# A two-layer attention and convolution encoder on one Trainium2 core: separate buffers for the convolution's first two accumulators

## The chip, the core and the metric

The kernel runs on one core of a Trainium2 chip. The core has a matrix engine (TensorE, in the profile PE, its weight loads PEld), a vector engine (VectorE, DVE), an activation engine (ScalarE, ACT), GpSimd (POOL), which here only issues transfers, and SyncE (SP), which issues the weight loads. Each engine works through its own queue in the order in which the program was written out for it. The metric is the device time of one execution, in microseconds; less is better.

## What is computed

Two layers over 512 tokens of width 1024, all in float32. Each layer is

```
x += 0.5 * SwiGLU(RMSNorm(x))
h  = RMSNorm(x); z = h @ W_in + b_in
     z = [q | k | v (3 head groups) | GLU input | 2 gates]
     A: dilated sliding-window attention of 3 groups, combined, projected
     B: u = a * sigmoid(g) -> depthwise convolution over 31 tokens -> LayerNorm -> Silu -> projected
x += (sigmoid(gate_A) * A + sigmoid(gate_B) * B) @ W_out
x += 0.5 * SwiGLU(RMSNorm(x))
x  = RMSNorm(x)
```

The change lies in branch B. The reference's convolution is, for each of the 1024 channels, a sum of 31 shifted and scaled copies of `u`, plus a bias.

## The kernel before, in words

Activations lie transposed, channels on the 128 partitions and the 512 tokens along the row, so that 1024 channels are eight tiles of 128x512. Every matrix product is made of three matmuls: both factors are split into a high and a low part (`hi`, `lo`; `xgh`, `xgl`; `zh`, `zl`), and `mm3` (lines 156 to 159) adds high x high, high x low and low x high in PSUM. Weights come in through `stage` (lines 140 to 154): SyncE loads 512 KB into `raw` (two buffers), ScalarE writes `hi` (line 152), VectorE writes `lo` (line 153; four buffers each).

`mixer` (from line 264) runs once a layer and does, in program order:

1. The GLU (lines 277 to 292): four chunks of two channel tiles. `ps_gg` and `ps_ga` are projected, scaled on VectorE (lines 287, 290), the gate goes through Sigmoid (line 288), and line 292 writes `u[k]`.
2. Three head groups: `tables` (lines 326 to 328), `qk_chunk` (lines 331 to 372), `v_chunk` and `attend` (lines 403 to 471). A unit of `attend` is scores on TensorE (424), a masked minimum on VectorE (437), Exp on ScalarE (443), transposes (446), a copy (448) and the product with V (454).
3. The two gates (lines 482 to 504), projected from the same `xgh`, `xgl` as the GLU and put through Sigmoid.
4. The convolution (lines 507 to 517), on VectorE alone: for each `k`, line 510 begins an accumulator `cv[k]` from `u[k]`, and line 516 adds the other 30 taps, one instruction each.
5. The LayerNorm over channels (lines 518 to 536): sum of the `cv` (520, 522), mean by a matmul with ones (524), subtraction (529), squares (184, 188), their sum (193), square root and reciprocal (198, 200), broadcast (207, 209), scaling (534), Silu (535), and the split of the result into `zh` and `zl` (166, 167). These two are written into the tags `xgh{k}` and `xgl{k}`, of which there is one buffer each.
6. The combination of the head groups (lines 539 to 578), whose results `y` are split into tiles of the tag `big`.
7. The projections of both branches (`ps_cp`, `ps_ap`), the merge, and the output projection.

The order on each engine is not the program's. A scheduler writes it out at compile time by a model of its own: an instruction with a smaller priority number (earlier in the program) goes first among those that are ready in the model, and later ones fill the holes. Two calls shift it: `stage` moves its three steps ahead by 150, and the LayerNorm (line 518) gets the priority of the point before the attention units, so that it goes ahead of units that are still waiting. A tile is taken from a ring of as many buffers as its tag has, and tiles of one tag take their buffers in program order; a tile whose buffer still has a reader waits for it. In the mixer the tag `big` serves `u[0]` to `u[7]`, then `cv[0]` to `cv[7]`, then the eight tiles of `y`, in this order, from `NB` = 10 buffers:

```
u[k] = slot("big", NB, name="u")                 # line 291
a = slot("big", NB, name="cv")                   # line 509
y.append(split(mp, acc, "big", NB))              # line 578
```

Of the kernel before, what the change touches and what calls it, by code (L numbers as in the profile page):

```python
# [44 lines left out]
def trunk(ctx: ExitStack, tc: tile.TileContext, A: dict, out: bass.AP):  # L45
# [79 lines left out]
    def pc(nm, l, k):  # L125
        i = VECS.index(nm) * 16 + l * 8 + k
        return pcol[:, i:i + 1]

    def cw(l, j, k):
        i = (l * CW + j) * 8 + k  # L130
        return cwc[:, i:i + 1]
# [4 lines left out]
    def uniq(s):  # L136
        cnt[0] += 1
        return f"{s}_{cnt[0]}"
# [22 lines left out]
    def split(pool, src, tag, bufs):  # L161

        return split_to(pool.tile([P, S], F32R, tag=tag, name=uniq("sh"), bufs=bufs), pool.tile([P, S], F32R, tag=tag, name=uniq("sl"), bufs=bufs), src)
# [100 lines left out]
    def mixer(l, xg, R, rr, after):  # L264
# [5 lines left out]
        with ExitStack() as mx:  # L270
            mp = mx.enter_context(tc.tile_pool(name=uniq("mix"), bufs=2))

            def slot(tag, bufs, dt=F32, name=None):
                return mp.tile([P, S], dt, tag=tag, name=uniq(name or tag), bufs=bufs)


            u = [None] * KD
            NB = 10
            for c in range(4):
                ga = [ps_mm(uniq("ps_ga")) for _ in range(2)]  # L280
                gg = [ps_at(uniq("ps_gg")) for _ in range(2)]
# [2 lines left out]
                for j in range(2):  # L284
                    k = 2 * c + j
# [4 lines left out]
                    nc.vector.tensor_mul(ta, ga[j], R)  # L290
                    u[k] = slot("big", NB, name="u")
                    nc.vector.scalar_tensor_tensor(u[k], ta, bcol[:, l * 32 + k:l * 32 + k + 1], s, op0=ALU.add, op1=ALU.mult)
# [24 lines left out]
            for i, (nm, f) in enumerate((("q_norm", SCALE), ("k_norm", -1.0))):  # L317
                a = A[nm]
# [164 lines left out]
            for c in range(4):  # L483
                ps = [ps_mm(uniq("ps_gc")) for _ in range(2)]
                proj_cols(win, 3 * AW + 3 * D + c * 256, xg, KD, ps)
                for j in range(2):
                    k = 2 * c + j
# [6 lines left out]
            for c in range(4):  # L494
# [4 lines left out]
                for j in range(2):  # L499
                    k = 2 * c + j  # L500
# [5 lines left out]

            cv = []
            for k in range(KD):
                a = slot("big", NB, name="cv")
                nc.vector.tensor_scalar(a, u[k], cw(l, 15, k), pc("conv_b", l, k), op0=ALU.mult, op1=ALU.add)  # L510
                for j in range(CW):
                    d = j - 15
                    if d == 0:
                        continue
                    t0, t1 = max(0, -d), min(S, S - d)
                    nc.vector.scalar_tensor_tensor(a[:, t0:t1], u[k][:, t0 + d:t1 + d], cw(l, j, k), a[:, t0:t1], op0=ALU.mult, op1=ALU.add)  # L516
                cv.append(a)
# [46 lines left out]
            for pr in range(4):  # L564
                acc = None
                for g in range(NG):
# [9 lines left out]
                    else:  # L576
                        nc.vector.tensor_add(acc, acc, o)
                y.append(split(mp, acc, "big", NB))

            for c in range(4):  # L580
                ps = [(ps_at if c % 2 else ps_mm)(uniq("ps_cp")) for _ in range(2)]
                proj_cols(wcp, c * 256, z, KD, ps)
                for j in range(2):
                    k = 2 * c + j
                    nc.vector.scalar_tensor_tensor(sgc[k], ps[j], pc("b_conv_proj", l, k), sgc[k], op0=ALU.add, op1=ALU.mult)
            mg = []
            for c in range(4):
# [3 lines left out]
                for j in range(2):  # L591
                    k = 2 * c + j
# [49 lines left out]
    for l in range(DEPTH):  # L642
        nxt, sq = [], [None]
        ffn(l, A["ffn1_w_up"], A["ffn1_w_down"], xg, R, collect("mix_norm", l, nxt, sq), deferred)
        xg, rc, R = nxt, sq[1], sq[2]
        nxt, sq = [], [None]
        mixer(l, xg, R, rc[0], collect("ffn2_norm", l, nxt, sq))
        xg, rc, R = nxt, sq[1], sq[2]

# [104 lines left out]
```

## Time and profile before

| | |
|---|---|
| median of three runs | 2701.04 us (2699.03 to 2702.19) |
| the profiled execution, device time | 2701.68 us |
| its span in the profile | 2699.7 us |
| instructions in the span | 30972 |
| first mixer, second mixer | about 385 to 1000 us, about 1725 to 2335 us |
| busy in the span: PE, DVE, ACT | 97%, 59%, 37% |

The span is the time from the first to the last instruction that the profile holds, and the device time has some 2 us around it. A busy share counts the time in which an engine executes something. Views of stretches give, for each, the busy time of every engine with its number of instructions, the granted clock of TensorE as a share of full speed (PEclk), the busy share of the transfer engines and the rate at which they moved data. A timeline gives one engine's instructions in order: start, duration, engine, line, operation, what is written from what, how many were merged, and in brackets how long the engine was idle before and whom it waited for.

### The profile page before, as it was taken

Reading aid. Unit: us, or ns where it says so; the run is one execution under the profiler, and the core shown is the slowest. Engines: PE = TensorE matmul, PEld = TensorE weight load, DVE = VectorE, ACT = ScalarE, POOL = GpSimd, SP = SyncE. Lnnn points to the kernel's source line nnn. Section 1 sums busy time; section 2 is a strip of 40 time slices with the busy share of each in tenths; the row PEclk is TensorE's granted clock in tenths of the full one; section 3 lists DMA queues with packets and bytes.
Section 4 is the critical chain, followed back from the end, with each engine's and each line's share of the span. In section 5 each row is a group of like instructions: output and inputs, shape, how many; then the busy total and the mean of one; then the engine's idle time right before and its main releaser. Section 6 shows DMA issues by size and latency. Waiting matters only on the chain.

```text
span 2699.7 us, 30972 instructions
## 1 busy us (share of the span) xinstructions
PE 2629.4 (97%) x12125; PEld 2133.9 (79%) x12125; DVE 1602.0 (59%) x2606; ACT 1005.0 (37%) x1568; POOL 110.7 (4%) x208
## 2 busy tenths in 40 slices
PE   8999999998998999999999999999989989999998
PEld 6888888776776788888888888887767767888887
DVE  4443344999997654443454433459999976534432
ACT  5332232244576242332332322323344862423222
POOL 1000000001011000000000000001011100000000
PEclk9999999998998999999999999999989989999999
DMA  5332233332333333332333323324234323333322
GB/s 157 94 98 94 94 109 98 89 107 87 118 102 96 109 94 95 100 94 94 102 94 94 100 91 97 108 84 127 80 96 124 103 82 115 94 101 95 96 96 74
DMA packets 253777, 268.64 MB, mean 100 GB/s; under 512 B 11624, under 2 KB 238320, under 8 KB 253632
## 3 DMA queue, kind: packets, MB, share of 16 engines
q1 hardware_dynamic: 242112, 234.91, 28.2%
q0 software_dynamic: 11504, 31.76, 4.0%
q8 instruction: 95, 1.56, 0.2%
q14 instruction: 50, 0.41, 0.1%
q10 hardware_dynamic: 16, 0.00, 0.0%
HBM read 251.75 MB, written 14.88 MB: 99 GB/s over the span
## 4 chain that ended last, share of the span: by engine, by line
PE 88%; DVE 9%; issue 1%; DMA 1%; ACT 1%; SPq 0%; POOL 0%; DVEq 0%; ACTq 0%; POOLq 0%
PE ps_a L159 6%; PE ps_a L158 6%; PE ps_b L157 6%; PE ps_d L159 6%; PE ps_b L158 6%; PE ps_b L159 6%; PE ps_d L158 6%; PE ps_d L157 6%; PE ps_a L157 6%; DVE cv L516 3%; PE ps_n L158 3%; PE ps_n L157 3%; PE ps_n L159 3%; PE ps_S L424 1%; PE ps_pv L454 1%
## 5 line engine op out<-in xcount | busy, mean ns | idle before, releaser
L153 DVE TENSOR_TENSOR lo<-raw,hi 128x1024 fp32r<-128x1024 f32 (+1 forms) x448 | 538.9, 1203 | 734.9 <-ACT hi L152 733.3
L152 ACT ACTIVATE hi<-raw 128x1024 fp32r<-128x1024 f32 (+1 forms) x448 | 468.1, 1045 | 1014.8 <-issue 349.6
L516 DVE SCALAR_TENSOR_TENSOR cv<-u,cwc,cv 128x497 f32<-128x497 f32 (+14 forms) x480 | 334.9, 734 | 0.1
L158 PE MATMUL ps_b<-xgl,hi 128*128 128x512 f32 x704 | 275.3, 391 | 0.0
L159 PE MATMUL ps_a<-xgh,lo 128*128 128x512 f32 x704 | 274.7, 390 | 0.0
L157 PE MATMUL ps_a<-xgh,hi 128*128 128x512 f32 x704 | 273.7, 390 | 0.8 <-ACT xgh L174 0.8
L158 PE MATMUL ps_a<-xgl,hi 128*128 128x512 f32 x704 | 274.4, 390 | 0.1
L157 PE MATMUL ps_b<-xgh,hi 128*128 128x512 f32 x704 | 274.2, 390 | 0.0
L159 PE MATMUL ps_b<-xgh,lo 128*128 128x512 f32 x704 | 274.1, 389 | 0.0
L157 PE MATMUL ps_d<-sh,hi 128*128 128x512 f32 x704 | 274.1, 389 | 0.0
L158 PE MATMUL ps_d<-sl,hi 128*128 128x512 f32 x704 | 274.1, 389 | 0.0
L159 PE MATMUL ps_d<-sh,lo 128*128 128x512 f32 x704 | 274.0, 389 | 0.0
L158 PE MATMUL ps_n<-lo,xgh 128*128 128x512 f32 x576 | 229.1, 398 | 4.0 <-DVE lo L153 3.8
L159 PE MATMUL ps_n<-hi,xgl 128*128 128x512 f32 x576 | 225.4, 392 | 0.0
L157 PE MATMUL ps_n<-hi,xgh 128*128 128x512 f32 x576 | 215.8, 395 | 6.5 <-DVE tmp L379 4.3
L157 PEld LDWEIGHTS ps_a<-xgh,hi 128*128 128x128 f32 x704 | 132.1, 188 | 28.7 <-ACT xgh L174 1.2
L159 PEld LDWEIGHTS ps_b<-xgh,lo 128*128 128x128 f32 x704 | 132.2, 188 | 28.1 <-issue 0.7
L158 PEld LDWEIGHTS ps_b<-xgl,hi 128*128 128x128 f32 x704 | 132.2, 188 | 28.0 <-issue 0.7
L158 PEld LDWEIGHTS ps_a<-xgl,hi 128*128 128x128 f32 x704 | 132.2, 188 | 27.8 <-DVE xgl L175 0.5
L159 PEld LDWEIGHTS ps_a<-xgh,lo 128*128 128x128 f32 x704 | 132.2, 188 | 27.6 <-issue 0.2
L158 PEld LDWEIGHTS ps_d<-sl,hi 128*128 128x128 f32 x704 | 132.2, 188 | 27.5
L157 PEld LDWEIGHTS ps_d<-sh,hi 128*128 128x128 f32 x704 | 132.2, 188 | 27.4
(234 smaller groups left out, 4001.7 us busy)
## 6 DMA issues: line engine op xcount, KB each, us to landing
raw<-in_ffn_w_up_dram SPq DMA_DIRECT2D x176, 512.0 KB, 3.5
raw<-in_w_in_dram SPq DMA_DIRECT2D x88, 512.0 KB, 3.6
raw<-in_ffn_w_down_dram SPq DMA_DIRECT2D x76, 512.0 KB, 3.5
raw<-in_w_in_dram SPq DMA_DIRECT2D x96, 256.0 KB, 3.1
raw<-in_w_conv_proj_dram SPq DMA_DIRECT2D x16, 512.0 KB, 3.5
raw<-in_w_out_dram SPq DMA_DIRECT2D x16, 512.0 KB, 3.5
vd<-tmp POOLq DMA_DIRECT2D x24, 256.0 KB, 2.4
od<-ot POOLq DMA_DIRECT2D x24, 256.0 KB, 3.1
```

Of the source, the lines that this page charges most:

```text
L152: nc.scalar.activation(hi[:, :m], raw[:, :m], AF.Copy)
L153: nc.vector.tensor_sub(lo[:, :m], raw[:, :m], hi[:, :m].bitcast(F32))
L157: nc.tensor.matmul(ps, ah, bh, start=first, stop=False)
L158: nc.tensor.matmul(ps, ah, bl, start=False, stop=False)
L159: nc.tensor.matmul(ps, al, bh, start=False, stop=last)
L424: nc.tensor.matmul(pS[e][:, w * n + lo:w * n + hi], qkT[hp, i, b * P:(b + 1) * P], qkT[hp, 2 + i, k0 + lo:k0 + hi], start=True, stop=True)
L454: nc.tensor.matmul(pv[e * 64:(e + 1) * 64, i, b - b2, :], V[b + j][:, (hh * UH + h) * HD:(hh * UH + h + 1) * HD], PT[e][:, (nj * w + j) * ...
L516: nc.vector.scalar_tensor_tensor(a[:, t0:t1], u[k][:, t0 + d:t1 + d], cw(l, j, k), a[:, t0:t1], op0=ALU.mult, op1=ALU.add)
```

## The change

The accumulators of the first two channel tiles take their buffers from a tag of their own, `cv`, with two buffers, and `big` has eight instead of ten. Nothing else differs.

```diff
             u = [None] * KD
-            NB = 10
+            NB = 8
...
             cv = []
             for k in range(KD):
-                a = slot("big", NB, name="cv")
+                a = slot("cv", 2) if k < 2 else slot("big", NB, name="cv")
                 nc.vector.tensor_scalar(a, u[k], cw(l, 15, k), pc("conv_b", l, k), op0=ALU.mult, op1=ALU.add)
                 for j in range(CW):
```

## Rows read from the trace of the kernel before

**Rows 1.** The page's busy times, with share of the span and instructions.

```profile
PE 2629.4 (97%) x12125; PEld 2133.9 (79%) x12125; DVE 1602.0 (59%) x2606; ACT 1005.0 (37%) x1568; POOL 110.7 (4%) x208
```

**Rows 2.** Stretches: length, PE, PEld, DVE, ACT, POOL busy; PEclk, DMA share, GB/s.

```profile
403.00:468.00 65.00, 65.00 (x288) 53.88 (x287) 28.21 (x33) 19.43 (x21) 0.00 (x0) 1.00 0.34 102
468.00:545.00 77.00, 72.71 (x322) 58.48 (x321) 76.79 (x132) 19.40 (x28) 4.86 (x9) 1.00 0.33 101
...
760.00:842.00 82.00, 82.00 (x455) 63.76 (x453) 72.54 (x158) 61.86 (x122) 9.80 (x18) 1.00 0.31 94
...
853.90:874.20 20.30, 10.15 (x25) 6.63 (x25) 13.83 (x33) 14.43 (x22) 0.76 (x1) 0.58 0.15 50
2190.80:2208.70 17.90, 10.18 (x26) 6.43 (x26) 13.38 (x31) 15.05 (x24) 1.85 (x3) 0.62 0.22 73
643.00:675.00 32.00, 23.61 (x132) 16.67 (x129) 31.17 (x70) 16.13 (x41) 2.38 (x4) 0.73 0.10 26
```

**Rows 3.** Timeline of VectorE, first layer's GLU and convolution start.

```profile
398.19 0.43 DVE L326 TENSOR_TENSOR tab<-rt,gqk 128x256 f32<-128x256 f32 x1
...
402.62 0.74 DVE L292 SCALAR_TENSOR_TENSOR u<-tmp,bcol,tmp 128x512 f32<-128x512 f32 x1
...
467.44 0.75 DVE L292 SCALAR_TENSOR_TENSOR u<-tmp,bcol,tmp 128x512 f32<-128x512 f32 x1
468.11 1.00 DVE L510 TENSOR_SCALAR cv<-u,cwc,pcol 128x512 f32<-128x512 f32 x2
```

**Rows 4.** Timeline of TensorE, from the last gate matmul on, first layer.

```profile
853.71 0.39 PE L159 MATMUL ps_gA<-xgh,lo 128*128 128x512 f32 x1
858.03 1.84 PE L193 MATMUL ps_ss<-ones,sq 128*128 128x1 f32 x8 [3.94 <-DVE sq L188]
861.44 2.05 PE L209 MATMUL ps_bc<-dg,ones 128*128 128x512 f32 x2 [1.57 <-DVE dg L207]
866.34 1.22 PE L157 MATMUL ps_cp<-zh,hi 128*128 128x512 f32 x2 [2.85 <-ACT zh L166]
869.36 0.80 PE L158 MATMUL ps_cp<-zl,hi 128*128 128x512 f32 x1 [1.80 <-DVE zl L167]
```

**Rows 5.** Stretches, line 516 alone: length, DVE busy; PEclk, DMA share, GB/s.

```profile
772.00:840.00 68.00, 40.22 (x59) 1.00 0.30 88
```

**Rows 6.** Timelines of ScalarE and VectorE, splits of z and y.

```profile
865.67 0.61 ACT L166 ACTIVATE zh<-cv 128x512 fp32r<-128x512 f32 x1
...
874.41 0.69 DVE L167 TENSOR_TENSOR zl<-cv,zh 128x512 fp32r<-128x512 f32 x1
...
890.29 0.61 ACT L166 ACTIVATE sh<-oin 128x512 fp32r<-128x512 f32 x1
```

**Rows 7.** Stretches, the tile ps_cp alone: length, PE, PEld, DVE; PEclk, DMA.

```profile
853.90:874.20 20.30, 6.06 (x14) 4.34 (x15) 0.00 (x0) 0.58 0.15 50
2190.80:2208.70 17.90, 6.89 (x15) 4.97 (x16) 0.00 (x0) 0.62 0.22 73
```

**Rows 8.** Waits of TensorE from 468 to 545 us: total, times, longest.

```profile
PE ps_n L158 <- DVE lo L153: 1.4, 2, 1.0
PE ps_n L157 <- ACT hi L152: 1.1, 1, 1.1
```

**Rows 9.** Groups of ScalarE from 842 to 880 us: count, busy, mean ns, idle before.

```profile
L535 ACT ACTIVATE cv<-cv,pcol 128x512 f32<-128x512 f32 x8 | 6.1, 801 | 2.8 <-DVE cv L534 2.8
...
L184 ACT ACTIVATE sq<-cv 128x512 f32<-128x512 f32 x8 | 4.5, 626 | 0.4 <-DVE sq L188 0.4
```

**Rows 10.** Timeline of ScalarE around a table load.

```profile
759.26 1.10 ACT L371 ACTIVATE qkT<-ps_qT 128x512 f32<-128x512 f32 x1
760.38 1.28 ACT L490 ACT_TABLE_LOAD   x1
761.68 0.72 ACT L490 ACTIVATE sgc<-sgc,bcol 128x512 f32<-128x512 f32 x1
```

## The prediction

> **What bounds the kernel now.** I read the busy shares first. TensorE works in 97% of the span and VectorE in 59% [rows 1], so an edit that adds, drops and resizes no instruction can gain only where TensorE waits or runs at a lowered clock. Next I read the table of stretches around the first mixer [rows 2]. While the GLU is projected (403 to 468 us) TensorE is busy for all of the 65 us and VectorE for 28.2, so VectorE has 36.8 us free. Straight after, from 468 to 545, VectorE is busy for 76.8 of 77 us and TensorE loses 4.3. From 760 to 842, beside the last attention units, TensorE is full again, with ScalarE at 61.9 of 82 us. The loss that matters stands in the two short rows at the end of each mixer, 853.9 to 874.2 and 2190.8 to 2208.7: TensorE is busy for about half of them, at a granted clock of 0.58 and 0.62 of full speed (half speed, 1.2 GHz, for most of it). Another loss lies at 643 to 675, at 0.73.
>
> The VectorE timeline tells why the convolution begins when it does. `u[0]` is being written from 402.62, but the convolution's first instruction, line 510, is the one right behind the last `u` of line 292, at 468.11 behind 467.44 [rows 3]; the second layer shows the same order. Yet the rotary tables of line 326, which stand after the GLU in the program, ran at 398.19. So VectorE does run ahead of program order, and what held `cv[0]` is its place in the ring: ten `big` buffers, eight of them promised to `u[0]` to `u[7]` first.
>
> The timeline of TensorE at the end of the mixer shows who waits for the convolution's end. The last gate matmul starts at 853.71. Then come only the LayerNorm's own small steps, each after a wait: 3.94 us for the sum of squares, 1.57 for the diagonal, 2.85 for `zh`, 1.80 for `zl` [rows 4]. The rest of the convolution stands directly ahead of this chain: 59 of line 516's 240 instructions of the first layer lie between 772 and 840 us [rows 5].
>
> **The change, part by part.** It alters no instruction. *Buffers:* 10 `big` become 8 `big` and 2 `cv`, the same memory. *Moved:* `cv[0]` and `cv[1]`, per layer 2 of line 510 and 60 of line 516, may start behind `u[0]`, near 403 us instead of 468. At the pace of the convolution's packed stretch (59 in 40.2 us, 0.68 each [rows 5]) the 60 are 41 us, and with line 510's two (1.00 [rows 3]) 42 us. The free 36.8 us hold nearly all of it. *Queues:* SP's weight loads and POOL's loads keep their order, since no DMA moves. But a weight load waits until line 153 has read a `raw` buffer, and line 153 will now find convolution instructions ahead of it on VectorE. Two `raw` and four `hi`/`lo` buffers cover that. If the cover fails, TensorE waits. *`y`:* its second pair now follows `cv[2]` and `cv[3]` in the ring, not `cv[0]` and `cv[1]`. The `zh` that free these start from 865.67 us, `y`'s first split only at 890.29 [rows 6], so I cost this at nothing. Without that cover it would be two more z pairs, under 3 us.
>
> *Where the 42 us go.* The scheduler puts the convolution, last in priority, into VectorE's holes. With 62 instructions gone from the front, the later ones move up into the same holes, and the convolution ends 62 instructions earlier in the order, near 770 us instead of just before 840. The LayerNorm has the priority of the attention units, so its mean, squares, scaling and Silu come next, beside attention and the gate projections, which keep TensorE busy. Only the split into `zh`, `zl` cannot move: it writes the buffers `xgh`, `xgl`, which the last gate matmuls read until 854. So the output projection of the convolution (`ps_cp`) can follow the gates almost directly, and not earlier.
>
> *Gain.* At full clock a projection matmul takes 0.226 us (288 in 65 us [rows 2]). The first stretch of 20.3 us holds 15 `ps_cp` matmuls by their weight loads [rows 7], 3.4 us, and the LayerNorm's ten, 3.9 us as they stand in rows 4, about 1.9 at full clock. Lost: 20.3 - 3.4 - 1.9 = 15.0. The second: 17.9 - 16 x 0.226 - 1.9 = 12.4. Together 27.4 us.
>
> *What stays or is added, per layer.* (a) A saturated VectorE during the GLU. The nearest rows are those of 468 to 545, where line 153 cost TensorE 1.4 us and its partner on ScalarE 1.1 [rows 8]: 2.5 x 65/77 = 2.1. Bounds: 0, as the GLU shows now, and 3.6 (all 4.3 us of that stretch). I take 2.1, as the waits of rows 8 are of the GLU's own kind. (b) The LayerNorm's small matmuls may still wait inside attention: 0 to 3.94 + 1.57 = 5.5. I take 1.5, about one of the shorter waits, since TensorE now comes to them with other work in hand. (c) The first z pair behind the gates: 0 to 2.85 + 1.80 = 4.6. I take 1.3, one `zh` and one `zl` (0.61 + 0.69 [rows 6]), since the Silus ahead of them are done by then. Sum 4.9, for both layers 9.8.
>
> Net gain: 27.4 - 9.8 = 17.6. The profiled execution took 2701.68 us (span 2699.7 and 2.0 around it), 0.6 above the median of the three runs, 2701.04. 2701.7 - 17.6 = 2684.1, or 2683 against the median. With all costs at zero it is 2674; with all at their upper ends (13.7 per layer) the gain is nil.
>
> **The rivals.** *More gain (2654).* The stall of 643 to 675 is also VectorE running late: 8.4 us idle, and 14.8 with the clock's share on 23.6 busy us (0.27 of them) [rows 2]. If convolution instructions no longer stand there, up to two times 14.8 come on top: 2654. Against it: convolution instructions from further back move up into those very holes, as everywhere else.
>
> *The LayerNorm stays last (2703).* If the convolution only spreads thinner and still ends beside the last attention unit, nothing of the 27.4 is gained and (a) costs up to 4.2: 2701 to 2705. For it: the holes are the scheduler's, not the trace's. Against it: VectorE has no idle time to spread over between 468 and 545 [rows 2].
>
> *It doesn't begin earlier (2701).* Something other than the ring could hold the convolution. Rows 3 speak against it: line 510 comes in the very slot behind the last `u`.
>
> *ScalarE becomes the bound (2713).* The LayerNorm lands in 760 to 842, where ScalarE has 20.1 us left [rows 2]. Its squares and Silus are 10.6 us [rows 9], which leaves 9.5. Sqrt and Silu need other function tables than attention's Exp. A table load starts 0.02 us after the instruction before it has ended, and the next activation starts 1.30 us after the load (760.38 to 761.68 [rows 10]). Taken together, one Sqrt and eight Silus in a row need 4 loads, 5.2 us: it fits. If each Silu falls between two Exps it is up to 18 loads, 23.4 us: 13.9 us over. From the eighth load on (9.5/1.30 = 7.3) attention is late, and TensorE with it. An idle microsecond costs 1.48 with the lowered clock behind it (15.0 lost for 10.15 idle in rows 2). The gain of 8.8 a layer is gone at 5.9 us over, 12 loads; at 15 loads it is 10.0 us over, 14.8 lost a layer, 29.6 - 17.6 = 12 us slower. For it: the load pairs already stand around the gates' Sigmoids. Against it: the Silus come with the higher priority, so in a row.
> The Trainium skill (ScalarE: Activation LUTs, sections "What ACT_TABLE_LOAD costs" and "Table sets: the hidden batching unit") speaks for this rival: group calls by table set, since each switch is priced at a load of 1283 ns and a drain of 1380 ns, 2.66 us. By that figure the least case, 4 loads, would be 10.6 us, 1.1 over, and the sum 2687; by rows 10 the load agrees and the drain does not show, so the measurement decides.
>
> **How the numbers follow.** A measurement of this kernel can tell about 0.2%, 5.4 us, from no change. Chances: forecast 0.58, more gain 0.10, LayerNorm last 0.12, not earlier 0.05, ScalarE 0.15. Faster: 0.58 and 0.10, less 0.01 for the forecast's costs at their upper ends, 0.67. Same: 0.05, that 0.01, and 0.09 of the LayerNorm case, 0.15. Slower: ScalarE's 0.15 and 0.03 of the LayerNorm case with (a) above its bound, 0.18. The forecast's own range is 2674 to 2694. The range of 8 in 10 reaches down to the larger gain, 2654, and up over the unchanged cases to 2703; ScalarE's case and a little at either end stay out.
>
> **What would show it.** Right: line 510 starts near 403 us, VectorE is full between 403 and 468 with TensorE still above 62 of 65; the last line 516 ends some 60 us before the last gate matmul; line 535's Silus stand before it too, and `ps_cp` follows it within 3 us at full clock. Wrong: `ps_mu` still behind the last attention unit (LayerNorm last); more than seven table loads added beside the last units, with TensorE waiting for `sp` or `PT` (ScalarE); line 510 still behind the last `u` (not earlier). Waits of `ps_gg` or `ps_ga` for line 153 above 4 us a layer would sink term (a).

## The result, and the profile after

| | before | after |
|---|---|---|
| median of four runs | 2701.61 us (2699.03 to 2702.52) | 2668.97 us (2668.5 to 2670.5) |
| the profiled execution's span | 2699.7 us | 2667.5 us |
| mean granted clock of TensorE | 0.984 | 0.992 |

The ratio is 0.9882, with a 95% interval of 0.9865 to 0.9899: 32.6 us less, a gain clearly over 0.2%. The forecast was 2683 us, its own range 2674 to 2694. The sign, the mechanism and the outer range held; the time lies 5 us below the forecast's own range, the gain is nearly twice the 17.6 us of the sum, and lies between the forecast's case and that of "more gain".

The busy times of the page after, against [rows 1]:

```profile
PE 2617.8 (98%) x12125; PEld 2125.9 (80%) x12125; DVE 1599.7 (60%) x2606; ACT 1005.8 (38%) x1572; POOL 110.5 (4%) x208
```

The same instructions, but for four table loads more on ScalarE (six more in the first layer, two fewer in the second). So the time came out of TensorE's idle time (span less busy time, 70.3 before and 49.7 after) and of its clock (11.6 us less busy for the same matmuls). Where, the stretches of after say (columns as in [rows 2]):

```profile
405.00:468.00 63.00, 63.00 (x280) 52.18 (x279) 62.94 (x90) 16.56 (x18) 0.00 (x0) 1.00 0.33 101
468.00:545.00 77.00, 72.60 (x324) 58.64 (x323) 75.89 (x130) 19.70 (x29) 4.88 (x10) 1.00 0.34 100
...
760.00:842.00 82.00, 79.58 (x440) 61.98 (x435) 48.51 (x126) 79.03 (x146) 10.08 (x19) 1.00 0.27 86
640.00:680.00 40.00, 31.58 (x184) 23.13 (x184) 38.31 (x83) 21.68 (x47) 4.00 (x7) 0.79 0.13 35
```

And the same cuts of before, as far as [rows 2] does not have them:

```profile
405.00:468.00 63.00, 63.00 (x279) 52.21 (x278) 26.31 (x30) 18.02 (x19) 0.00 (x0) 1.00 0.33 101
640.00:680.00 40.00, 31.61 (x184) 23.04 (x183) 38.36 (x83) 21.54 (x47) 4.00 (x7) 0.79 0.12 33
```

During the GLU VectorE goes from 26.31 to 62.94 busy us of 63, and TensorE does not notice: 63.00 both times. From 468 to 545 nothing changes, nor does the stall around 640 to 680. From 760 to 842 VectorE is relieved (72.54 to 48.51) and ScalarE fills up (61.86 to 79.03); TensorE loses 2.4 us there that it did not lose before.

VectorE's timeline after, against [rows 3]: the start of the convolution, its last taps, and the sum for the mean:

```profile
402.55 0.74 DVE L292 SCALAR_TENSOR_TENSOR u<-tmp,bcol,tmp 128x512 f32<-128x512 f32 x1
403.20 0.69 DVE L290 TENSOR_TENSOR tmp<-ps_ga,R 128x512 f32<-128x512 f32 x1
403.81 0.54 DVE L510 TENSOR_SCALAR cv<-u,cwc,pcol 128x512 f32<-128x512 f32 x1
...
772.24 1.38 DVE L516 SCALAR_TENSOR_TENSOR cv<-u,cwc,cv 128x497 f32<-128x497 f32 x2
773.53 0.68 DVE L489 TENSOR_TENSOR sgc<-ps_gc,R 128x512 f32<-128x512 f32 x1
774.13 0.68 DVE L522 TENSOR_TENSOR tmp<-tmp,cv 128x512 f32<-128x512 f32 x1
```

Line 510 now stands behind `u[0]` and not behind `u[7]`. The last tap ends at 773.6; before, taps ran up to 840 [rows 5].

TensorE's timeline after, the LayerNorm's mean and the end of the gates, against [rows 4]:

```profile
778.79 1.02 PE L524 MATMUL ps_mu<-tmp,ones 128*128 128x512 f32 x2
...
856.79 0.39 PE L159 MATMUL ps_gA<-xgh,lo 128*128 128x512 f32 x1
857.02 0.60 PE L561 MATMUL ps_cT<-ident,cg 128*96 128x128 f32 x4
857.38 0.48 PE L157 MATMUL ps_cp<-zh,hi 128*128 128x512 f32 x1
857.69 0.39 PE L158 MATMUL ps_cp<-zl,hi 128*128 128x512 f32 x1
```

The chain of single waits of [rows 4] is gone. `ps_cp` stands 0.6 us behind the last gate matmul, at full clock, and no row of it has a bracket. The second layer shows the same, at 2174.10 and 2174.68.

Behind that point lies a gain that the prediction has no term for. Stretches from there to the last `ps_cp` matmul; before, from the ends of the two gaps on:

```profile
874.20:926.90 52.70, 50.39 (x208) 38.80 (x207) 32.93 (x48) 12.18 (x16) 4.30 (x8) 0.90 0.35 109
2208.70:2259.50 50.80, 48.31 (x206) 36.67 (x205) 31.91 (x50) 11.57 (x15) 4.30 (x8) 0.97 0.36 113
```

After, from the first `ps_cp` on:

```profile
857.40:908.60 51.20, 51.20 (x218) 38.09 (x216) 33.08 (x44) 13.26 (x17) 4.30 (x8) 1.00 0.39 128
2174.70:2227.50 52.80, 52.80 (x219) 39.16 (x217) 32.55 (x44) 12.47 (x16) 4.30 (x8) 0.97 0.38 120
```

After, all 192 `ps_cp` matmuls are done in these stretches; before, 15 and 16 of them were done already in the gaps [rows 7]. At 0.226 us each, what the stretches hold beside `ps_cp` is 52.7 - 177 x 0.226 = 12.7 and 50.8 - 176 x 0.226 = 11.0 before, 51.2 - 192 x 0.226 = 7.8 and 52.8 - 43.4 = 9.4 after: 6.5 us less. The clock is higher in the first layer (0.90 to 1.00) and the same 0.97 in the second. What the rest was, TensorE's waits over the whole run say (us in total, times, longest). Before:

```profile
PE ps_c L569 <- DVE oin L573: 2.5, 2, 1.6
PE ps_cp L157 <- DVE oin L573: 2.3, 1, 2.3
```

After, no wait for `oin` is left; the two longest that remain, and the only one of the LayerNorm, are:

```profile
PE ps_T L446 <- ACT sp L443: 11.8, 8, 2.9
PE ps_pv L454 <- ACT PT L448: 9.8, 14, 1.1
...
PE ps_bc L209 <- DVE dg L207: 0.6, 2, 0.3
```

### The profile page after: what moved, and what is told of

Read it like the earlier page. It is cut to its first block, busy times and chain, and to the rows that moved or that the text cites. A ratio compares the mean times of both kernels' runs of the same rounds, so it can differ in the third digit from the quotient of the medians.

```text
span 2667.5 us, 30985 instructions
## 1 busy us (share of the span) xinstructions
PE 2617.8 (98%) x12125; PEld 2125.9 (80%) x12125; DVE 1599.7 (60%) x2606; ACT 1005.8 (38%) x1572; POOL 110.5 (4%) x208
## 4 chain that ended last, share of the span: by engine, by line
PE 88%; DVE 7%; ACT 3%; issue 1%; DMA 0%; SPq 0%; ACTq 0%
PE ps_a L158 6%; PE ps_a L159 6%; PE ps_b L157 6%; PE ps_d L157 6%; PE ps_b L158 6%; PE ps_b L159 6%; PE ps_d L159 6%; PE ps_d L158 6%; PE ps_a L157 6%; PE ps_n L158 4%; PE ps_n L157 4%; PE ps_n L159 3%; DVE cv L516 2%; PE ps_cp L158 1%; PE ps_cp L159 1%; PE ps_cp L157 1%
## 5 line engine op out<-in xcount | busy, mean ns | idle before, releaser
L516 DVE SCALAR_TENSOR_TENSOR cv<-u,cwc,cv 128x500 f32<-128x500 f32 (+14 forms) x480 | 335.7, 737 | 0.1
L159 PEld LDWEIGHTS ps_d<-sh,lo 128*128 128x128 f32 x704 | 132.2, 188 | 27.5
L157 PEld LDWEIGHTS ps_b<-xgh,hi 128*128 128x128 f32 x704 | 132.2, 188 | 27.4
```

What stands on the lines that cost most here:

```text
L157: nc.tensor.matmul(ps, ah, bh, start=first, stop=False)
L159: nc.tensor.matmul(ps, al, bh, start=False, stop=last)
```

## The experiments

Each kernel ran beside the kernel before: the first four on one chip (before: 2701.18, 13 runs), the last four on another (before: 2703.3, 9 runs). The kernel after did not run again beside them: differences from it are those of the medians, and by the ratios they come out up to some 2 us otherwise. Diffs are against the kernel after, but for one.

**The new rings without the early start.** The bias of line 510 is read, for the first two tiles, from a column that needs `u[7]`. Buffers are as after, the start as before.

```diff
+                cb = pc("conv_b", l, k)
+                if k < 2:
+                    hb = rp.tile([P, 1], F32, tag="hb", name=uniq("hb"), bufs=2)
+                    nc.vector.tensor_scalar(hb, u[7][:, 0:1], 0.0, cb, op0=ALU.mult, op1=ALU.add)
+                    cb = hb
-                nc.vector.tensor_scalar(a, u[k], cw(l, 15, k), pc("conv_b", l, k), op0=ALU.mult, op1=ALU.add)
+                nc.vector.tensor_scalar(a, u[k], cw(l, 15, k), cb, op0=ALU.mult, op1=ALU.add)
```

> The changed kernel (8 big, 2 cv), but line 510 of cv[0] and cv[1] takes its bias from a small column that is computed from u[7] (times 0, plus the bias), so that both begin only after the last u. Theory (the gain is the early start alone): back at the kernel before, 2698 to 2704 us, first line 510 near 468 us, ps_mu behind the last attention units. Rival (the ring of eight and y's new places in it bring the gain): stays at 2669.

2708.06 us (ten runs, 2705.08 to 2712.23), ratio 1.0025 [1.0015, 1.0034]. The first accumulator starts at 470.62, behind the last `u`. The gain is gone whole: it is the early start, not how the rings share the memory. The gates ended 4.6 us earlier than before, and the wait behind them grew by 5.1, from 3.94 to 9.07. TensorE's timeline of this kernel:

```profile
849.09 0.39 PE L159 MATMUL ps_gA<-xgh,lo 128*128 128x512 f32 x1
858.55 1.86 PE L193 MATMUL ps_ss<-ones,sq 128*128 128x1 f32 x8 [9.07 <-DVE sq L188]
...
866.89 1.22 PE L157 MATMUL ps_cp<-zh,hi 128*128 128x512 f32 x2 [2.85 <-ACT zh L166]
```

So while the LayerNorm is last, time won ahead of it is waited off again. Why the kernel is 7 us slower than before is not settled; its profiled execution, the fastest of the ten, is 3.2 slower, of which 0.6 are there when `ps_cp` starts.

**Half of the move.** One accumulator in a ring of its own.

```diff
-            NB = 8
+            NB = 9
-                a = slot("cv", 2) if k < 2 else slot("big", NB, name="cv")
+                a = slot("cv", 1) if k < 1 else slot("big", NB, name="cv")
```

> Only cv[0] has a buffer of its own (9 big, 1 cv): half of the moved work. Theory (a threshold: what counts is that the LayerNorm's Silus are done when the last gate matmul is): the convolution ends about 30 instructions earlier than before, near 805 us, the LayerNorm takes 41 us in the changed kernel (ps_mu 779 to last Silu 820), so it is done near 846, still ahead of the gates' end at 857: nearly the whole gain, 2669 to 2675 us. Rival (in proportion to the work moved): 2685.

2669.53 us, ratio 0.9885 [0.987, 0.9899]: the whole gain with half of the move. The stretch of the GLU in this kernel:

```profile
405.00:468.00 63.00, 63.00 (x279) 52.17 (x278) 46.96 (x62) 17.18 (x19) 0.00 (x0) 1.00 0.33 101
```

And the mean's matmuls in both layers (durations, first and last start):

```profile
L524 PE MATMUL ps_mu<-tmp,ones x4: 592/644/697, 814.0 to 2134.8; 128*128 128x512 f32 x4
```

VectorE does about half of the added work early (46.96, between 26.31 and 62.94). The mean comes 35 us later than after, and `ps_cp` starts at 856.36 none the less, 1.0 earlier than after. Right behind, TensorE waits 1.0 us for the second split (0.80 for `zh`, 0.23 for `zl`): here the LayerNorm ends just in time.

The gain is not in proportion to the work moved. The rows fit a threshold: what counts is that the LayerNorm ends before the gates' matmuls do, and from then on more work in the early hole buys nothing. This is the one kernel between none and all of the move.

**Taps left out, to empty the stall.** In each layer 90 of the 240 taps of line 516 (all of tiles 6 and 7, half of 4 and 5) are not computed.

```diff
-                    if d == 0:
+                    if d == 0 or k > 5 or (k > 3 and j > 15):
```

> The changed kernel without line 516 for k = 6 and 7 and without the taps above 15 for k = 4 and 5, so that the convolution is over before 640 us; it leaves out 90 of 240 taps a layer. It asks what the remaining stall near 643 to 675 us is made of. Theory (convolution instructions queued ahead of line 437 on VectorE): the waits of ps_T for sp (5.3 us) there go, and with the clock up to 14 us a layer: 2640 to 2650 us. Rival (the bare latency of the attention units, for which TensorE has no other work there): 2662 to 2669.

2651.05 us, ratio 0.9814 [0.9798, 0.9831]: 17.9 below after. This takes work off VectorE outside the stall too; the next kernel does not.

**The taps moved instead.** All taps are computed, but those of tiles 4 and 5 from the twentieth on wait, through the column that holds the weight, for the last masked minimum (line 437) of head group 0's second half.

```diff
+                    w = cw(l, j, k)
+                    if k in (4, 5) and j == 19:
+                        hw = rp.tile([P, 1], F32, tag="hw", name=uniq("hw"), bufs=2)
+                        nc.vector.tensor_scalar(hw, g0st[1][:, 3, 3:4], 0.0, w, op0=ALU.mult, op1=ALU.add)
+                        w = hw
```

> The changed kernel, full work, but from the 19th tap on cv[4] and cv[5] wait (through a small column computed from st) for the last line 437 of head group 0, so that no convolution instruction stands between 645 and 668 us; some 30 of them move behind it. Theory (they cause the stall): the stall loses most of its 14 us a layer, the convolution ends some 20 to 30 us later (near 805), the LayerNorm still hides for the most part: 2645 to 2660 us. Rival (bare latency): no gain there, 2669 or up to 10 more, since the LayerNorm comes later.

2664.51 us, ratio 0.9863 [0.9848, 0.9878], 4.5 below after, with overlapping intervals. The stall's stretch in the kernel without the taps (first) and in this one (second), against 31.58 and 0.79 after:

```profile
640.00:680.00 40.00, 35.22 (x239) 26.82 (x238) 21.16 (x62) 24.66 (x51) 4.55 (x8) 1.00 0.27 76
```

```profile
640.00:680.00 40.00, 34.95 (x234) 26.56 (x233) 27.94 (x72) 25.03 (x52) 4.54 (x8) 1.00 0.25 74
```

In both the clock stays at its upper level, and TensorE's wait for `sp` in this stretch falls from 5.3 to 1.2 us; its wait for `PT`, 3.0, stays. So the lowered clock and some 3.4 of the 8.4 idle us of the stall come from taps that VectorE does ahead of attention's masked minima, as the rival "more gain" had it, and the change leaves them as they were. In the second kernel the gates' last matmul starts at 846.63, 10.2 earlier than after, yet little of it arrives: from the first to the last `ps_cp` it takes 56.5 us (after: 51.2), at a clock of 0.94, with the wait for `oin` back (the shifted line numbers are the same steps):

```profile
PE ps_c L578 <- DVE oin L582: 4.5, 4, 1.3
```

**More buffers for `oin`.** The next three runs put two of five `oin` tiles into the ring `ot` and three into `sp`, which is free by then. First on the kernel before:

```diff
-                    o = slot("ot", 4, name="oin")
+                    i = pr * NG + g
+                    o = slot("ot", 4, name="oin") if i % 5 < 2 else slot("sp", 6, name="oin")
```

> The kernel before, but the twelve oin loads of a layer take turns in the ring ot (4) and the idle ring sp (6), so that up to ten of them can be under way instead of four. Between its first full-speed output-projection matmul and its last, TensorE spends 12.7 and 11.0 us on other things than these matmuls, the changed kernel 7.8 and 9.4. Theory (the 6.5 us of gain that the prediction did not count are waits behind line 569 for oin): with early loads they go here too, 2690 to 2697 us. Rival (they come from the order in which the scheduler lays ps_c between ps_cp): 2699 to 2703.

2693.44 us, ratio 0.9963 [0.995, 0.9975]: the waits for `oin` and the lowered clock behind them cost the kernel before some 10 us. In the profiled executions the way from the first to the last `ps_cp` is 8.4 us shorter in sum (55.9 and 55.5 us in the two layers; before, 60.5 and 59.3). Then on the kernel after, where these waits are gone:

> The same edit of the loads on the changed kernel. Theory: little is left to gain there, 2664 to 2669 us, and the distance to the kernel before with the same edit shrinks to about 26 us. Rival: 2669, distance unchanged at 32.

2675.06 us, ratio 0.9896 [0.9882, 0.9909]. Against before that is 28.2 us, against 32.6 of the kernel after; the intervals overlap, so a loss is not proved, but there is no second gain to be had. Beside the kernel before with the same edit the change is worth 18.4 us, where 32.6 less the missing 6.5 would leave 26; the falls of the clock shown here are part of the rest. Both expectations missed what the profiled execution shows (2678.35, the longest of four runs from 2672.13): it is 8.9 us longer than after's, 6.2 of them from the first to the last `ps_cp` (56.0 and 54.3 in the two layers, against 51.2 and 52.8). Two stretches of it:

```profile
875.00:880.00 5.00, 5.00 (x15) 3.62 (x15) 3.79 (x7) 0.00 (x0) 0.43 (x1) 0.66 0.51 157
...
885.00:890.00 5.00, 5.00 (x12) 3.34 (x13) 3.19 (x6) 0.63 (x1) 0.00 (x0) 0.54 0.23 79
```

After, the same cuts stand at 1.00. No wait ends there; TensorE is busy throughout, and a matmul takes longer:

```profile
875.12 0.56 PE L570 MATMUL ps_c<-tmp,sel 8*128 8x512 f32 x1
875.61 0.80 PE L158 MATMUL ps_cp<-zl,hi 128*128 128x512 f32 x1
876.21 0.63 PE L159 MATMUL ps_cp<-zh,lo 128*128 128x512 f32 x1
876.63 0.63 PE L157 MATMUL ps_cp<-zh,hi 128*128 128x512 f32 x1
```

Last on the kernel with the moved taps:

> The paused convolution and the early oin loads together. The paused kernel gained about 10 us by the gates' end in the first layer and gave half of it back behind line 569 (waits for oin 5.8 us in all, and the clock at half speed after them). Theory: with the loads early it keeps more, 2652 to 2660 us. Rival (the give-back is not the loads): 2662 to 2665.

2650.38 us, ratio 0.9806 [0.9792, 0.9819]. First to last `ps_cp` takes 50.5 us instead of 56.5, at full clock, and in the second layer 52.1 instead of 57.9, at 0.97. The waits of `ps_c` for `oin` are gone, 1.5 us of `ps_cp` stay. The kernel is 18.6 us below the kernel after (20.5 by the ratios). It computes all that the kernel before does, and beats both.

**ScalarE relieved.** The gates' Sigmoids (lines 490, 503) become plain copies: no Sigmoid, no bias, and none of their table switches.

```diff
-                    nc.scalar.activation(s, s, AF.Sigmoid, bias=bcol[:, l * 32 + 24 + k:l * 32 + 25 + k])
+                    nc.scalar.activation(s, s, AF.Copy)
```

> The changed kernel with Copy in place of the Sigmoids of lines 490 and 503 (it leaves out both gates' Sigmoid and bias), so that no function table is changed for them beside the last attention units. ScalarE is busy for 39.7 of 40 us there (800 to 840). Theory (TensorE has the gates to fill in, so the full ScalarE costs it only the 2 to 3 us that it is idle there): 2664 to 2669 us. Rival (ScalarE has become the bound of this stretch): 2655 to 2661.

2664.92 us, ratio 0.986 [0.9845, 0.9876], 4 to 6 us below after by the median and by the ratio, and the intervals just overlap. The stretch where ScalarE is fullest, after (first) and here (second):

```profile
800.00:840.00 40.00, 37.85 (x210) 28.75 (x210) 18.80 (x56) 39.69 (x78) 6.53 (x12) 1.00 0.27 86
```

```profile
800.00:840.00 40.00, 40.00 (x220) 30.80 (x217) 20.30 (x66) 29.23 (x66) 5.83 (x11) 1.00 0.33 105
```

With 10.5 us less on ScalarE TensorE wins back 2.15; in the second layer (2120 to 2160) it is 1.26. By the last gate matmul the profiled execution, the fastest of its four, is 5.4 us ahead of after's (851.4 against 856.8), of which 1.5 stand before the first gate. So ScalarE does hold attention there after the change, for 2 to 4 us in the first layer and less in the second, and is not the bound.

## Why the prediction was right in kind and short in size

**The mechanism held at each step.** Line 510 starts at 403.81 (said: near 403). VectorE is full during the GLU and TensorE untouched. The convolution ends at 773.6 (said: near 770). The LayerNorm then runs beside the last units and the gates, its mean at 778.8. `ps_cp` follows the last gate matmul within 0.6 us at full clock (said: within 3). Only the distance from the last tap to the last gate matmul was said too short: 83 us, not some 60. The first experiment shows that the early start is the cause, the second that the gain comes as soon as the LayerNorm is no longer last.

**The gross gain of 27.4 was right.** Both gaps are closed. The gates' end moved by 856.79 - 853.71 = 3.1 us in the first layer. In the second it went from 2190.6 to 2174.1, 16.5 earlier, where the whole stream is 18.3 earlier by the end of the first layer's `ps_cp` (926.9 to 908.6): 1.8 later. Of each, 1.9 are the LayerNorm's own matmuls (the prediction's estimate), which the gain already left out.

**The step that failed is the sum of costs, (a) to (c): 9.8 taken, 1.1 measured** (3.1 - 1.9 and 1.8 - 1.9). The 1.1 is a difference of positions and no sum of waits: in the first layer TensorE waits 2.0 us for `sp` and `PT` from 760 to 842, which belong to the ScalarE rival and to none of the three terms.
- (a), 2.1 a layer for a saturated VectorE during the GLU, was 0. The waits for `lo` and `hi` of [rows 8] were the nearest rows, but they did not come with the saturation: from 385 to 640 TensorE waits 1.6 us for `lo` before and after, and 1.1 and 1.3 for `hi`. The `raw`, `hi` and `lo` buffers that the prediction named as cover held at 62.94 busy us of 63.
- (b), 1.5 a layer, was 0.3: only `ps_bc` still waits inside attention, twice 0.3 us.
- (c), 1.3 a layer, was 0: the splits that the first `ps_cp` matmuls need stand before the gates' end, the first three `zh` at 851.38. The prediction put them all behind it. Not all eight pairs are needed at once, and by tile `k` the buffers fall free while the last gate still reads the later ones. ScalarE's row:

```profile
851.38 1.66 ACT L166 ACTIVATE zh<-cv 128x512 fp32r<-128x512 f32 x3
```

**A term that was missing: 6.5 us.** The prediction ended its view at 874.2 and 2208.7, the ends of the gaps. Behind them `ps_c` and `ps_cp` waited for `oin`, and the clock fell once more (0.90 and 0.97; after, 1.00 and 0.97). That more buffers for `oin` give the kernel before 10 us, and the kernel after none, shows that the loss was there and that the change had taken most of it. What released it was not tried by itself. VectorE is no freer there, busy for 0.64 of 857 to 909 after and for 0.63 of 866 to 927 before. What differs is how far apart the twelve pairs of `ps_c` stand, which the four `oin` buffers have to serve (durations, first and last start; before, then after):

```profile
L569 PE MATMUL ps_c<-tmp,sel x12: 392/492/501, 885.4 to 899.6; 8*128 8x512 f32 x12
```

```profile
L569 PE MATMUL ps_c<-tmp,sel x12: 391/492/501, 863.9 to 885.2; 8*128 8x512 f32 x12
```

They are spread over 21.3 us instead of 14.2. In the kernel with the moved taps they stand within 16.3 (861.2 to 877.5), and the waits are back. The rows fit with that; it is not shown by an experiment. 27.4 - 1.1 + 6.5 = 32.8, against 32.2 of the spans.

**The rivals.** "LayerNorm last" and "not earlier" are refuted by the timelines above. "More gain" had its mechanism right and did not come: the stall stands unchanged because later taps move up into the same holes, which was the argument against it. Moving the taps out by hand is worth some 18 to 20 us, and only with the next wait, that for `oin`, removed too; its two times 14.8 were too much, as 5 us of the 40 stay idle with the taps gone, 3.0 of them for `PT` and 1.2 for `sp`.

"ScalarE becomes the bound" was the closest call. Its engine did fill, to 39.69 of 40. ScalarE's timeline after, around the Silus:

```profile
810.73 1.28 ACT L535 ACT_TABLE_LOAD   x1
812.02 0.82 ACT L535 ACTIVATE cv<-cv,pcol 128x512 f32<-128x512 f32 x1
...
815.71 4.34 ACT L535 ACTIVATE cv<-cv,pcol 128x512 f32<-128x512 f32 x6
820.06 1.28 ACT L443 ACT_TABLE_LOAD   x1
821.35 0.40 ACT L443 ACTIVATE sp<-sp,st 128x128 f32<-128x128 f32 x1
```

The eight Silus share one load, as the least case had it. In the prediction's stretch, 760 to 842, there are 18 loads, where before 11 stood: seven more. Four are the LayerNorm's, three come from the gates' Sigmoids, which change places with attention's Exps more often. That is one under the eight from which attention was to be late by the prediction's count. The threshold was near the truth, as TensorE had begun to wait there, 2.0 us for `sp` and `PT`. In the second layer there are two loads fewer than before, and from 2000 to 2200 TensorE waits 1.0 us for `sp` and `PT`, before 2.2. The Trainium skill (ScalarE: Activation LUTs, section "What ACT_TABLE_LOAD costs") prices each switch at 2.66 us, a load and a drain, and by that figure seven more would be 18.6 us, an estimate. This trace agrees with the page on the load, 1.28 us, but shows only 1.29 from its start to the next activation (810.73 to 812.02) and no drain, so the measurement decides.

## What to carry to other kernels

Where tiles of one ring take buffers in program order, look for a tile that could be computed early and is held by promises to earlier tiles; whether to free it is read at the other end, at what waits last for its results. Such a gain can be a threshold, as here: take the smallest move that brings the late chain under its cover, and do not charge a saturated engine as a cost where its buffers cover the lag. When a gap closes, follow the profile past it: the same late engine may hold the next stretch too, and time won ahead of a late wait is waited off there until that wait goes as well.

## What the runs showed that was not expected

A lowered clock without a wait. In the kernel after with more `oin` buffers, the granted clock fell to 0.66 and 0.54 of two 5 us stretches in which TensorE counts as busy for all of it. Each stands behind eight small `ps_c` matmuls (8 rows) that alternate with full ones, from 872.60 to 875.12 and from 882.01 to 885.75.

The kernel after shows it too, in its second layer. This is the stretch with the fall (0.66 from 2190 to 2195, 1.00 on both sides):

```profile
2190.00:2200.00 10.00, 10.00 (x34) 6.42 (x33) 7.03 (x12) 1.69 (x2) 2.15 (x4) 0.83 0.61 185
```

It stands behind a run of eight from 2188.64 to 2191.16. In the first layer of the same kernel the same run, at the same spacing, stands from 871.33 to 873.85, and the clock stays up. The kernel with moved taps and more buffers has no fall in its first layer, and one to 0.66 in its second (2184 to 2189), behind twelve small ones and a wait of 0.74. So the order of small and large matmuls alone does not decide it, and what lowers the clock stays open.
